# One step of a hybrid decoder on eight cores: rows transposed once and kept on chip, sample attention in small units, cache copies moved to the FFN

## Chip, cores, metric

The kernel runs on all 8 cores of one Trainium2 chip (two dies of four cores). The metric is the device time of the slowest core in microseconds (us). The four runs of the kernel before agree within 0.3% (2707.73 to 2713.84 us). Engines: PE is TensorE (PEld its weight loads), DVE is VectorE, ACT is ScalarE, POOL is GpSimd, SP is SyncE; with a "q" behind it, an engine's name stands for its issuing of instructions and DMAs. SBUF and PSUM are the on-chip memories in which the code places its tiles; `PS` in the code is PSUM. The granted clock is what the profile records of TensorE's clock, as a share of full speed. A unit, a slot and a pass are the program's own terms and are explained with the change.

## The reference, cut to what matters

```
BATCH, SEQ, D_MODEL = 4, 2048, 2048; DEC_BATCH, DEC_SEQ = 32, 4
DIL_GROUPS = ((128, 1), (512, 4), (2048, 16))   # (window, dilation), 4 heads of 128 each
D_CONV, CONV_WIDTH, FFN_HIDDEN = 1024, 31, 5632

h = rms_norm(x, g_mix)
z = h @ w_in                                    # [glu | q | k | v | gate_conv | gate_attn]
u = glu[..., :D_CONV] * sigmoid(glu[..., D_CONV:])
q, k = rope(...), rope(...)                     # rotary on 32 of 128 columns
conv_out = silu(layer_norm(depthwise_conv31(u))) @ w_pw
o_att = attention of 3 dilated groups, combined by their softmax denominators
        # prompt: each position and 128 earlier ones at stride 1, 4, 16
        # sample: 4 new rows per sequence against the cache; returns the caches shifted by 4 rows
x = x + (gate_conv * conv_out + gate_attn * (o_att @ w_o_att)) @ w_out
x = x + (silu(hf @ w_gate) * (hf @ w_up)) @ w_down     # hf = rms_norm(x)
```

A core takes 1024 prompt positions with 1024 earlier ones as halo (their keys and values are computed again), and four sample sequences (16 rows).

## The kernel before: the parts concerned

For every 128-row block of every group, the rows of x are loaded again, normalised and transposed, and Q, K, V are projected one after the other. The helper `S` records every operation for its engine and derives waits from the regions of SBUF and PSUM that an operation touches.

```python
def do_norm(idx):
    norm_tile(src, skey, hblk, 'hblk')
    ...
    issue_xload(nl)                       # next block's rows of x, stride d
    if bi_ >= 4:
        issue_copy_piece()                # cache copies, beside the x loads
        issue_copy_piece()

def do_block(idx, cur):
    ...
        do_norm(nxt)
    if has_q:
        proj(7, hTb[xi], hkey, 2)         # 16 matmuls of 512 columns each
    proj(0, hTb[xi], hkey, 0)
    proj(1, hTb[xi], hkey, 1)
    ...                                   # rope, casts, transposes of q and k
    do_T(nxt)                             # 16 transposes of the next block's rows
    for ki, (kbuf, mi) in enumerate(keyblocks):
        for h in range(4):
            S.op('pe', ... matmul(PS[sb_], lhsT=kT, rhs=qT ...))
            S.op('pe', ... matmul(PS[sb_], lhsT=identb, rhs=mb ...))   # the mask
        S.op('act', ... AF.Exp ...)
    ...

for idx, (g, bi_, r, b, kind) in enumerate(allblocks):
    if bi_ == 0:
        wload(2, w_in[...Q of g...]); wload(0, ...K...); wload(1, ...V...)
    do_block(idx, cur)
# then: sample attention, a stage of its own (VectorE passes of 2048 columns)
# then: for t in range(10): a3_norm(t) ...   rows loaded, normalised, transposed once more
# then: GLU and convolution, layer norm, gates, output projection, FFN
```

The waits come from this rule, which is the same in both kernels. Note the divisions by 32: two writes into different partitions of the same group of 32 count as a conflict.

```python
def region(self, ap):
    ...
    q0, q1 = p0 // 32, (p0 + ap.ap[0][1] + 31) // 32
```

The softmax here doesn't subtract the row's maximum and nothing guards it: scores larger than these inputs give would overflow.

## Time and profile before

| | before |
|---|---|
| time | 2708.93 us in the median of four (2707.73 to 2713.84) |
| setup and prompt attention | 0 to 737 us |
| sample attention | 737 to 905 us |
| second normalisation and transposition | 905 to 960 us |
| GLU and convolution | 960 to 1213 us |
| layer norm | 1213 to 1278 us |
| gates, wait for output weights, output projection, FFN | 1278 to 2709 us |

The boundaries are read from the timeline at the first and last instruction of each stage. The lines behind them are in the prediction below: the slices, the windows of these stages and the chain of waits. The share of busy time over the whole span (PE 84%) says little here; each stage has its own limit.

### The profile page before, as it was taken

Reading aid. Unit: us, or ns where it says so; the run is one execution under the profiler, and the core shown is the slowest. Engines: PE = TensorE matmul, PEld = TensorE weight load, DVE = VectorE, ACT = ScalarE, POOL = GpSimd, SP = SyncE. Lnnn points to the kernel's source line nnn. Section 1 sums busy time; section 2 is a strip of 40 time slices with the busy share of each in tenths; the row PEclk is TensorE's granted clock in tenths of the full one; section 3 lists DMA queues with packets and bytes.
Section 4 is the critical chain, followed back from the end, with each engine's and each line's share of the span. In section 5 each row is a group of like instructions: output and inputs, shape, how many; then the busy total and the mean of one; then the engine's idle time right before and its main releaser. Section 6 shows DMA issues by size and latency. Waiting matters only on the chain.

```text
span 2708.9 us, 36511 instructions; the slowest of 8 cores (2694.7 to 2708.9 us)
## 1 busy us (share of the span) xinstructions
PE 2277.3 (84%) x14139; PEld 1285.9 (47%) x14139; DVE 940.9 (35%) x1417; ACT 569.9 (21%) x1035; POOL 121.4 (4%) x123
## 2 busy tenths in 40 slices
PE   1894885798744389997999949999999999999997
PEld 0451443344311245554666624556555665556663
DVE  1441533354477532214222212432333223332215
ACT  1451432343432421115111101300000000000012
POOL 0000000000000000000110000000000000000000
PEclk9996997898956589998999979999999999999999
DMA  9598799694364413330546576555535546446413
GB/s 196 116 188 135 162 200 183 128 202 128 58 150 150 149 18 47 46 47 1 68 64 84 75 191 85 84 87 76 81 63 76 80 65 91 64 66 91 63 32 126
DMA packets 207406, 272.00 MB, mean 100 GB/s; under 512 B 5785, under 2 KB 185369, under 8 KB 196255
## 3 DMA queue, kind: packets, MB, share of 16 engines
q0 software_dynamic: 185712, 127.93, 34.0%
q1 hardware_dynamic: 21525, 141.74, 20.5%
q8 instruction: 115, 1.88, 0.3%
q14 instruction: 54, 0.44, 0.1%
HBM read 381.86 MB, written 59.99 MB: 163 GB/s over the span
## 4 chain that ended last, share of the span: by engine, by line
PE 78%; DMA 9%; DVE 5%; ACT 4%; issue 3%; another core or an unknown queue 1%; SPq 0%; ACTq 0%; DVEq 0%; POOLq 0%
PE ps L219 78%; DMA t_62<-w_in 3%; DMA t_69<-xext 2%; DMA wf_151<-w_out 2%; DVE t_99 L219 1%; DVE t_106 L219 1%; DMA t_59<-vecs 1%; DVE t_97 L219 0%; DMA t_117<-xext 0%; ACT t_89 L219 0%; ACT t_124 L219 0%; ACT t_71 L219 0%; ACT junk__179 L219 0%; ACT t_73 L219 0%
## 5 line engine op out<-in xcount | busy, mean ns | idle before, releaser
L219 PE MATMUL ps<-t_113,t_61 128*128 128x347 bf16 (+3 forms) x1152 | 186.6, 315 | 1.2 <-ACT t_143 L219 1.2
L219 PE MATMUL ps<-t_113,t_62 128*128 128x347 bf16 (+3 forms) x1152 | 183.4, 312 | 0.0
L219 ACT ACTIVATE sgb_177<-ps 128x347 f32<-128x347 f32 (+1 forms) x66 | 30.3, 459 | 537.8 <-PE ps L219 537.8
L219 PEld LDWEIGHTS ps<-t_113,t_61 128*128 128x128 bf16 x1152 | 112.4, 98 | 63.7 <-issue 1.8
L219 PEld LDWEIGHTS ps<-t_113,t_62 128*128 128x128 bf16 x1152 | 111.6, 97 | 60.1
L219 PE MATMUL ps<-t_61,t_72 128*128 128x512 bf16 x320 | 79.2, 405 | 45.9 <-DMA t_61<-w_in 45.0
L219 PE MATMUL ps<-t_142,wh_161 128*128 128x347 bf16 (+1 forms) x576 | 93.3, 316 | 0.5 <-DVE t_142 L219 0.5
L219 PE MATMUL ps<-t_63,t_73 128*128 128x512 bf16 x288 | 70.5, 402 | 25.5 <-DMA t_63<-w_in 21.9
L219 PE MATMUL ps<-t_142,wh_162 128*128 128x347 bf16 (+1 forms) x576 | 91.3, 312 | 0.0
L219 PE MATMUL ps<-t_142,wh_159 128*128 128x347 bf16 (+1 forms) x576 | 90.9, 311 | 0.0
L219 PE MATMUL ps<-t_142,wh_160 128*128 128x347 bf16 (+1 forms) x576 | 90.9, 311 | 0.0
L219 ACT ACTIVATE sgb_178<-ps 128x347 f32<-128x347 f32 (+1 forms) x66 | 30.3, 459 | 279.3 <-PE ps L219 279.3
L219 PE MATMUL ps<-t_62,t_72 128*128 128x512 bf16 x320 | 77.2, 397 | 12.1 <-DMA t_62<-w_in 12.1
L219 PE MATMUL ps<-t_61,t_73 128*128 128x512 bf16 x320 | 74.5, 387 | 9.4 <-DMA t_61<-w_in 7.5
L219 PE MATMUL ps<-t_114,t_63 128*128 128x347 bf16 (+1 forms) x384 | 66.7, 314 | 18.3 <-ACT t_114 L219 18.3
L219 PE MATMUL ps<-t_62,t_73 128*128 128x512 bf16 x320 | 75.1, 390 | 6.6 <-DMA t_62<-w_in 6.6
L219 PE MATMUL ps<-t_142,wh_157 128*128 128x347 bf16 (+1 forms) x480 | 75.7, 311 | 0.0
L219 PE MATMUL ps<-t_142,wh_158 128*128 128x347 bf16 (+1 forms) x480 | 75.7, 311 | 0.0
L219 PE MATMUL ps<-t_142,wh_156 128*128 128x347 bf16 (+1 forms) x480 | 75.7, 311 | 0.0
L219 PE MATMUL ps<-t_142,wh_155 128*128 128x347 bf16 (+1 forms) x480 | 75.7, 311 | 0.0
L219 PEld LDWEIGHTS ps<-t_61,t_72 128*128 128x128 bf16 x320 | 32.7, 103 | 89.0 <-issue 55.9
L219 DVE SCALAR_TENSOR_TENSOR t_71<-t_69,t_56,t_59 128x2048 bf16<-128x2048 f32 x19 | 44.7, 2352 | 86.4 <-ACT t_56 L219 86.4
(359 smaller groups left out, 3790.2 us busy)
## 6 DMA issues: line engine op xcount, KB each, us to landing
t_69<-xext SPq DMA_DIRECT2D x19, 1024.0 KB, 10.4
t_70<-xext SPq DMA_DIRECT2D x18, 1024.0 KB, 14.8
t_61<-w_in POOLq DMA_DIRECT2D x12, 1024.0 KB, 12.4
t_62<-w_in POOLq DMA_DIRECT2D x12, 1024.0 KB, 15.9
kso<-ck SPq DMA_DIRECT2D x8, 1016.0 KB, 23.1
vso<-cv SPq DMA_DIRECT2D x8, 1016.0 KB
t_63<-w_in POOLq DMA_DIRECT2D x3, 2048.0 KB, 29.0
t_61<-w_in POOLq DMA_DIRECT2D x3, 2048.0 KB, 38.5
```

The source lines that it names most:

```text
L219: self.q[eng].append(lambda e: getattr(e, meth)(*a, **kw).then_inc(s, 1))
```

## The change

Its intent is to give TensorE less to do and nothing to wait for in the first 1213 us. The 1024 own rows, the halo and the sample rows are normalised and transposed once, into `hT`, and stay on chip for all later stages. Each group becomes a pass for Q (its result kept as `qT`) and a pass for K and V, with masks as VectorE multiplies; a pass is a loop over blocks of 128 rows, and a slot is a place in such a loop at which other work may be put. The sample rows' Q, K, V are three matmuls side by side in column tiles. Sample attention is cut into 51 units (17 per group), each with its loads, three VectorE passes of 512 columns, one exponential and one matmul, spread over later stages: units 0 to 16 (group 0) run in group 1's passes, 17 to 33 in group 2's, 34 to 50 in the GLU stage. The cache copies are issued during the FFN. The core of the diff:

```diff
-        hblk = ab(o, 1024); o += 1024
-        hTb = [v3(ab(o, 1024), 16), v3(ab(o + 1024, 1024), 16)]; o += 2048
+        hT = v3(ab(H_, 16 * HP), 16)              # all rows, transposed, for all stages
...
+        def u_load(u):
+            if kind == 'n':                       # the new rows among themselves
+                for dst, r0, key in ((K_, 16, 1), (V_, 32, 2)):
+                    S.dma('sp', dst[0:64, :], ...)
+                for i_ in range(4):
+                    S.dma('sp', Q_[16 * i_:16 * i_ + 16, :], ...)
+                return
+            S.dma('sp', Q_, sq[4 * s + i:4 * s + i + 1, :].partition_broadcast(128), ...)
+            if g > 0 or i == 0:
+                S.dma('sp', K_, ck[g][s]...)
+                S.dma('sp', V_, cv[g][s]...)
+        def u_dve(u):
+            S.op('dve', ... tensor_tensor(out=P_, in0=K_, in1=Q_, op=ALU.mult))
+            S.op('dve', ... tensor_reduce(out=S_, in_=v3(P_, 4), axis=AX.X, op=ALU.add))
+            S.op('act', ... activation(out=pc, in_=S_, func=AF.Exp, scale=SCALE))
+            S.op('dve', ... tensor_tensor(out=v3(PV_, 4), in0=v3(V_, 4), in1=..pc.., op=ALU.mult))
+        def unit_slot(lim):                       # matmul of one unit, loads of the next, VectorE of one
...
+        def slotA0(i):                            # group 0: rows still to be normalised
+            if i < 6:
+                norm(11 + i)
+            if i < 7:
+                T(10 + i, 0, 7)                   # transposition into bank 7, then a copy on VectorE
+        def slotB0(i):
+            if i < 7:
+                T(10 + i, 1, 7)                   # same bank, copy on ScalarE
...                                               # GLU and convolution, per channel block n, slot ti
                     S.op('act', ... AF.Sigmoid ...)
                     S.op('dve', ... scalar_tensor_tensor(...))
                     if ti == 0:
                         S.op('dve', ... out=dg[ui] ...)   # 31 diagonals, 3968 columns
+                    unit_slot(50)
+                    if n == 1 and ti == 0:
+                        prompt_norm()             # reciprocal, then 8 x (matmul, multiply)
...                                               # FFN
+        def copy_slot():
+            slots[0] += 1
+            if slots[0] % 2 == 0 and copies:
+                d_, s_ = copies.pop(0)
+                S.dma('act', d_, s_)
```

## The prediction

> **What bounds the kernel now.** I read the page's slices first, to find where TensorE is not dense; then the windows view with boundaries I set at the stage changes that the timeline shows; then the chain of waits, for what fills the gaps; last the DMA queues.
>
> ```profile
> PE   1894885798744389997999949999999999999997
> PEclk9996997898956589998999979999999999999999
> DMA  9598799694364413330546576555535546446413
> ```
>
> One digit is 68 us. The right two thirds are a wall of nines at full clock. The losses are in the left third: slices 0, 3 to 6, and above all 11 to 14. In the windows below (busy us and count per engine, then clock, DMA share, GB/s) the first four are setup and the prompt attention of the groups 0, 1, 2; then sample attention; a second norm and transpose of the rows; GLU and convolution; gates; the wait for the output weights; the FFN without its last down round.
>
> ```profile
> 0.00:72.00 72.00, 9.12 (x35) 4.28 (x35) 10.67 (x16) 8.26 (x12) 3.76 (x7) 0.99 0.96 187
> 72.00:258.00 186.00, 138.32 (x905) 72.94 (x906) 62.52 (x130) 71.04 (x120) 3.43 (x3) 0.89 0.84 159
> 258.00:491.00 233.00, 172.25 (x1068) 90.06 (x1067) 88.50 (x167) 82.51 (x137) 3.43 (x3) 0.89 0.88 170
> 491.00:737.00 246.00, 213.24 (x1376) 110.12 (x1376) 109.64 (x237) 101.24 (x174) 4.17 (x4) 0.95 0.52 125
> 737.00:905.00 168.00, 72.92 (x258) 20.99 (x259) 118.50 (x63) 50.17 (x96) 0.40 (x1) 0.60 0.53 139
> 905.00:960.00 55.00, 17.85 (x168) 15.44 (x165) 28.12 (x18) 33.73 (x52) 0.00 (x0) 0.50 0.44 158
> 960.00:1213.00 253.00, 239.48 (x1546) 131.66 (x1546) 57.21 (x58) 29.35 (x75) 12.41 (x12) 0.98 0.31 39
> 1278.00:1573.00 295.00, 295.00 (x1999) 194.12 (x1999) 75.84 (x141) 42.25 (x94) 24.67 (x25) 1.00 0.53 67
> 1573.00:1617.00 44.00, 7.30 (x43) 3.90 (x40) 3.06 (x6) 0.86 (x2) 3.42 (x3) 0.64 0.95 249
> 1740.00:2635.00 895.00, 889.76 (x5574) 531.85 (x5574) 278.92 (x440) 64.12 (x138) 59.64 (x60) 1.00 0.50 75
> ```
>
> The chain (start, us, what) names what fills the gaps: at each change of group some 45 us for the weights plus 25 us for rows of x queued beside them; in sample attention one VectorE pass after the other.
>
> ```profile
> 169.87 13.76 PE ps L219 x97
> 211.86 43.98 DMA t_62<-w_in
> 377.73 23.52 DMA t_69<-xext
> 443.31 47.57 DMA t_62<-w_in
> 611.44 28.97 DMA t_69<-xext
> 779.99 2.30 DVE t_99 L219
> ```
>
> So TensorE bounds everything from 960 on (but for the wait of 44 us), TensorE and DMA share the attention, VectorE bounds 737 to 905, and a latency chain bounds 905 to 960.
>
> ```profile
> q0 software_dynamic: 185712, 127.93, 34.0%
> q1 hardware_dynamic: 21525, 141.74, 20.5%
> ```
>
> These two give transfer rates for saturated engines: casting weight loads 127.93 MB in 0.340 x 2709 = 921 us, 139 GB/s of bf16 (2.1 MB of weights cost 15 us); plain transfers 141.74 MB in 555 us, 255 GB/s (a 1 MB tile 4.1 us). I use them below.
>
> [...] The timeline has 16 such matmuls from 189.20 to 192.65 us, 0.2157 each[...]
> [...] mean clock 0.60 and 0.50 in the two stages with an idle TensorE. [...] 1.00 in gates and FFN with eight cores busy.
> [...] The change reads weights at strides 4 and 16; nothing before does, so the trace is silent.
> [...] x tiles land in 10.4 and 14.8 us in the median, against 5.0 us outside attention.
>
> **The change part by part.**
> *Rows normalised and transposed once.* 40 tiles in attention plus 10 before the convolution become 17. The stage 905 to 960 goes: **-55 us**. In attention 24 x 16 transposes at 0.055 us go, about 20 us of TensorE, and 21 reads of 1 MB of x.
>
> *Attention stages, rebuilt.* A projection is 16 x 0.2157 = 3.45 us. Before there are 37 K, 37 V, 32 Q and 9 sample projections (115); after 37 K, 37 V, 24 Q and three packed sample ones (48 matmuls of 32 columns; those of the FFN, 15 in 1.24 us, are packed the same way, so about 5 us each with their rope). 192 mask matmuls become VectorE multiplies. From the block of 13.76 us plus 1.3 us stall (period 15.05) I take small matmuls at 0.055 us.
> - q block: 3.45 + 4 transposes = 3.7 us. Its VectorE share: rope 0.9 (0.28 to 0.36 per op), copy 0.4.
> - full K/V block: 6.9 + 28 small x 0.055 = 8.5 us; g2 block (64 queries) 7.7; a block without queries 7.2.
> - VectorE per K/V block, with masks, rope, sums and one sample unit: 5.5 us, under the 8.5.
>
> *Group 0.* To the end of the q pass, DMA must bring three weights (45 us) and about 12.3 MB of x, gain and tables (48 us): 93 us, more than TensorE's 8 x 4.6 us. I take 92. Then 9 blocks x 8.5, 7 with a tile to transpose (0.9): 85, plus 5: **ends at 182** (before 258).
> *Group 1.* W0 is loaded early, W1 and W2 wait for the last block and take 30 us, while eight sample units bring 8 x 0.79 MB = 25 us: 54 us for a q pass that needs 30 on TensorE. Then 8 x 8.5 + 4 x 7.2 = 98, plus 5: 157, **ends at 339** (491).
> *Group 2.* 54 + 16 x 7.7 + 5 = 184, **ends at 523** (737).
> *Sample attention.* The 168 us stage goes. A unit has three VectorE passes over 512 f32 columns, a quarter of the 2.29 us passes each, 0.6, and waits 0.7 for the exponential: 2.6 us, 51 times, beside TensorE. On TensorE it costs one matmul of 0.22.
> *GLU and convolution.* 8 x 31 = 248 as before, + 17 units x 0.22 = 4, + normalising the prompt sums (8 f32 matmuls of 0.86, each with a VectorE pass of 0.69 and two handovers: 15, + reciprocal 3), + state transposes and last block 6: **276, ends at 799** (1213).
> *Sample normalisation, layer norm.* 65 + 7 = 72: 871 (1278).
> *Gates, wait for output weights, output projection, FFN.* Same instructions and the same buffer order: 295 + 44 + 123 + 969 = 1431: **2302**.
> *Cache copies.* 43.8 MB (2 x 4 x 2676 rows of 2 KB) leave attention and go, 172 us of DMA, into 8 of 11 FFN rounds of 85.5 us. The DMA share there goes from 0.50 to 0.75. Weights are loaded nearly a round ahead and land in 9 to 13 us, so I count nothing for it. For cold restarts of the clock and handovers not counted I add 13: **2315 us**.
>
> **The rivals.**
> *DMA latency becomes VectorE's wait.* Units load only one ahead, and VectorE takes its work in order: a unit whose keys are late holds up the rope, and so TensorE. For: three 256 KB loads per 3.7 us are 210 GB/s, beside weight loads. Against: only 16 slots lie in q passes; the K/V slots have 7 to 8 us. If each such slot takes 9 us: +35, 2350.
> *Strided weight loads become the bound.* The 512 loads of group 2 step 32 bytes. Contiguous loads keep up with 55 ns transposes, so a fourfold penalty just fits under 216 ns; more than that would add 50 to 100 us: 2365 to 2415.
> *The copies starve the FFN.* If loads double in latency and some arrive late: +20 to +60. Against it are the 0.75 and the slack of most of a round.
> *Gain hidden anyway.* If attention is DMA-bound throughout, fewer matmuls save little: from 0 to 523 there are 18.9 MB of weights (136 us) and by my estimate 46 MB of plain traffic (x 18, caches 10.5, queries 9, outputs 6.6, tables 2: 180 us), 316 of 523 us. So not on average, only at the group changes.
>
> **Range and chances.** The end of the convolution moves from 1213 to 799 (-414); layer norm gives back 7 and the allowance 13: -394, 2709 to 2315. Of it 223 us are two whole stages whose work has other engines' time to go to, which is why I am sure of the sign. Uncertain are the three q passes (each +-15), the GLU additions (+-12), strides (+0 to 60), copies (+0 to 50). Most errors make it longer: low 2260, high 2400. Slower or equal would take 340 us of new waits: faster 0.98, within 2% 0.015, slower 0.005.
>
> **What would show it right or wrong.** Right: attention ends at 500 to 560; no stage in which VectorE alone is dense; half clock only in the first 30 us, short spells at the group changes, layer norm and the output-weight wait; the FFN takes 969 us at clock 1.00 with a DMA share near 0.75; q passes of groups 1 and 2 near 54 us with W1 or W2 ending the wait. Wrong: weight loads of group 2 longer than 0.2 us with blocks over 8.5 us; VectorE waiting for cache keys inside K/V passes; waits for gate, up or down weights in the FFN.

## The result and the profile after

The changed kernel is correct. Of its four runs two were fast, at 2487.62 and 2488.5 us; the others (2542.23 and 2641.25 us) slow. Executions in which one die ran at a lower clock are left out of the means. The ratio to the kernel before is 0.9182, with a 95% interval from 0.9159 to 0.9204. A ratio here is the mean time of one kernel's fast runs over the mean of the other's in the same rounds, so it is not quite the ratio of medians. The kernel is 8.2% faster, 221 us; the forecast was 394 us, and the result lies outside the range of 2260 to 2400 us, 172 us above its centre.

The slices of the changed kernel (2487 us, so 62 us each), the counterpart of those in the prediction:

```profile
PE   3775996997577889699997598999999999999997
PEclk9888998998788899799999799999999999999999
DMA  9435427737132107047573956998889798544603
```

The gates, with which the dense wall begins, should have started at 871 us, in slice 14 (counted from 0); they start in slice 16, after a stretch of 5 to 8 in slices 10 to 14 in which the DMA row shows 0 to 3. No stage is VectorE's alone any more, and in the FFN, from slice 25 to 33, the DMA row rose to 7 to 9 with PE still at 9.

The windows of the same stages (us; busy and count of PE, PEld, DVE, ACT, POOL; clock; DMA share; GB/s): group 0's Q pass and K/V pass; group 1's start and rest; group 2's start and rest; the start of the GLU stage and its rest; the FFN.

```profile
39.00:105.00 66.00, 45.83 (x287) 23.70 (x285) 33.10 (x57) 29.92 (x49) 0.00 (x0) 0.88 0.77 176
105.00:218.00 113.00, 95.73 (x666) 49.77 (x667) 39.45 (x76) 41.92 (x72) 3.43 (x3) 0.91 0.30 72
218.00:260.00 42.00, 13.75 (x79) 6.56 (x78) 8.22 (x21) 3.29 (x8) 0.00 (x0) 0.67 0.90 162
...
387.00:424.00 37.00, 12.30 (x67) 6.07 (x66) 8.71 (x20) 2.33 (x6) 0.06 (x1) 0.68 0.98 171
424.00:591.00 167.00, 163.92 (x956) 102.79 (x955) 84.69 (x216) 28.22 (x70) 6.84 (x6) 0.98 0.50 107
591.00:666.00 75.00, 40.83 (x227) 21.53 (x225) 21.04 (x26) 16.33 (x24) 0.00 (x0) 0.77 0.61 109
666.00:973.00 307.00, 241.73 (x1328) 120.24 (x1328) 81.60 (x94) 59.44 (x96) 10.11 (x10) 0.86 0.23 45
...
1517.00:2412.00 895.00, 889.80 (x5574) 531.74 (x5574) 278.11 (x441) 64.13 (x138) 59.12 (x60) 1.00 0.74 124
```

The two dense passes (424 to 591, and the one before 387) are what the forecast promised (in the one before 387, from 260 us on, PE is busy for 126.55 of 127 us). Four windows are not: the K/V pass of group 0, the starts of groups 1 and 2 at a clock of two thirds, and above all the GLU stage, 382 us instead of 276, with TensorE at 0.77 and 0.86 of its clock although the DMA engines are busy to 0.61 and 0.23 only.

The chain of waits at the starts of groups 1 and 2 (start, us, what):

```profile
218.93 17.34 DMA t_67<-sqkv
236.99 6.69 DMA t_67<-sqkv
243.74 4.96 DMA t_67<-sqkv
...
467.55 12.80 DMA t_64<-ck
```

Where before 45 us for weights and 25 us for rows of x stood, there are now three loads in a row of the sample queries, `t_67`, 64 rows of 2 KB in all. They belong to the first unit of each group, the "new rows" unit, whose Q tile is written by four DMAs of 16 partitions. By the rule quoted above, the second waits for the first and the fourth for the third, because each of these pairs lies in one group of 32 partitions; the third is issued right behind the second, so three waits follow each other. The last line is a later wait, for a key tile of the cache, inside group 2's K/V pass. At the start of the GLU stage the same three take 13.36, 6.02 and 5.08 us.

Inside the GLU stage the timeline of one slot reads (start, us, engine, line, operation, operands, count, idle time before it and what ended that):

```profile
828.88 4.28 DVE L212 TENSOR_TENSOR t_105<-t_44,t_50 128x3968 bf16<-128x3968 bf16 x1
833.21 0.69 DVE L212 TENSOR_TENSOR t_69<-t_63,t_67 128x512 f32<-128x512 f32 x1
834.77 1.28 ACT L212 ACT_TABLE_LOAD   x1 [6.50 <-DVE t_75 L212]
836.28 1.28 ACT L212 ACT_TABLE_LOAD   x1
837.21 0.58 PE L212 MATMUL ps<-t_71,t_49 128*32 128x512 bf16 x1 [5.62 <-DVE t_71 L212]
```

VectorE first builds the 31 diagonals, 4.28 us, and only then starts the unit. ScalarE has to load the table of the exponential for the unit's four columns and, right behind it, the table of the sigmoid again. The unit's matmul stands in TensorE's order ahead of the next projection, so TensorE idles 5.62 us for it. The groups of table loads in the two kernels give the count:

```profile
L219 ACT ACT_TABLE_LOAD x8 | 10.3, 1283 | 36.1 <-PE ps L219 34.6 <-DVE t_137 L219 1.3
```

```profile
L212 ACT ACT_TABLE_LOAD x42 | 53.9, 1283 | 158.7 <-PE ps L212 78.0
```

The first is before (8 loads), the second after (42): the 34 that came to it are two for each of the 17 units of the GLU stage. ScalarE is 17% busy in the page of the changed kernel; that row hides them.

In the K/V pass of group 0, the timeline shows once per block:

```profile
132.79 0.67 PE L212 MATMUL ps<-t_44,t_61 128*128 128x128 bf16 x8 [3.02 <-DVE t_55 L212]
```

These eight transpositions write the PSUM bank whose former content VectorE has yet to copy; that copy (0.68 us, at 131.96) is queued behind a normalisation's multiply (2.35 us, at 129.69), which itself waits for ScalarE (2.85 us of idle time before it). After TensorE's 3.02 us of idle time the granted clock is 0.51, from 133.2 to 136.7 us, and the next projection takes 5.28 us instead of 3.63.

By stage, in us (forecast as lengths of the stages in the prediction; measured on the slowest core):

| stage | before | forecast | after | miss |
|---|---|---|---|---|
| start to the end of group 0 | 258 | 182 | 218 | +36 |
| group 1 | 233 | 157 | 169 | +12 |
| group 2 | 246 | 184 | 204 | +20 |
| sample attention, second normalisation | 223 | 0 | 0 | 0 |
| GLU and convolution | 253 | 276 | 382 | +106 |
| layer norm | 65 | 72 | 77 | +5 |
| gates to the end | 1431 | 1431 | 1437 | +6 |
| allowance | | 13 | | -13 |
| | 2709 | 2315 | 2487 | +172 |

### The profile page after: what moved, and what is told of

Same layout as the page of the kernel before. It is cut to its first block, busy times and chain, and to the rows that moved or that the text cites.

```text
span 2486.9 us, 34422 instructions; the slowest of 8 cores (2471.8 to 2486.9 us)
## 1 busy us (share of the span) xinstructions
PE 2164.7 (87%) x13264; PEld 1254.8 (50%) x13264; DVE 826.9 (33%) x1434; ACT 417.2 (17%) x789; POOL 121.6 (5%) x123
## 4 chain that ended last, share of the span: by engine, by line
PE 80%; DMA 8%; DVE 4%; issue 4%; ACT 3%; SPq 0%; DVEq 0%; ACTq 0%; POOLq 0%
PE ps L212 80%; DMA t_67<-sqkv 2%; DMA wf_141<-w_out 2%; DMA t_52<-w_in 1%; DMA t_68<-sqkv 1%; ACT L212 1%; DMA t_64<-ck 1%; DMA t_58<-xext 0%; DVE t_131 L212 0%; DVE t_130 L212 0%; ACT t_60 L212 0%; SPq L231 0%; ACT t_170 L212 0%; ACT t_112 L212 0%; DVE t_60 L212 0%
## 5 line engine op out<-in xcount | busy, mean ns | idle before, releaser
L212 PE MATMUL ps<-t_55,t_52 128*128 128x347 bf16 (+3 forms) x1152 | 189.8, 322 | 6.9 <-ACT t_133 L212 6.9
L212 PE MATMUL ps<-t_53,t_55 128*128 128x512 bf16 (+1 forms) x640 | 156.5, 401 | 6.0 <-DVE t_55 L212 6.0
L212 PE MATMUL ps<-t_55,t_53 128*128 128x347 bf16 (+3 forms) x960 | 153.7, 315 | 0.0
L212 PEld LDWEIGHTS ps<-t_55,t_52 128*128 128x128 bf16 x1152 | 115.6, 101 | 73.1 <-issue 9.1
L212 PE MATMUL ps<-t_54,t_55 128*128 128x512 bf16 (+1 forms) x640 | 145.1, 380 | 0.0
L212 PEld LDWEIGHTS ps<-t_55,t_53 128*128 128x128 bf16 x960 | 94.4, 99 | 51.1 <-issue 1.3
L212 PE MATMUL ps<-t_52,t_55 128*128 128x512 bf16 (+1 forms) x432 | 107.6, 407 | 11.8 <-DMA t_52<-w_in 11.8
L212 PEld LDWEIGHTS ps<-t_53,t_55 128*128 128x128 bf16 (+1 forms) x640 | 77.0, 126 | 68.9 <-issue 26.3
L212 PEld LDWEIGHTS ps<-t_54,t_55 128*128 128x128 bf16 (+1 forms) x640 | 76.7, 121 | 52.7
L212 ACT ACT_TABLE_LOAD x42 | 53.9, 1283 | 158.7 <-PE ps L212 78.0
L212 PEld LDWEIGHTS ps<-t_52,t_55 128*128 128x128 bf16 (+1 forms) x432 | 43.1, 104 | 63.5 <-issue 27.5
```

What stands on the lines that cost most here:

```text
L212: self.q[eng].append(lambda e: getattr(e, meth)(*a, **kw).then_inc(s, 1))
```

## The experiments

Theory: the gain was given back in four separate places: (a) the units in the GLU stage, through the alternation of tables and through their place behind the diagonals; (b) the four Q loads that wait for each other; (c) the order of copy and multiply in group 0; (d) the prompt normalisation, a chain of handovers. Rivals are the forecast's: DMA occupation, strided weight loads, starved FFN. Three kernels give a wrong sample output. "Gained" is the difference of a run's ratio to the changed kernel's 0.9182, times the 2709 us of before. The 95% intervals of the ratios are mostly 5 to 7 us wide to either side, so differences of a few us between gains mean nothing. The expectations took such differences from single runs; some of their figures differ from those here by a few us (95 us in place of 87 for the units left out).

### The units of the GLU stage left out (wrong)

```diff
-                    unit_slot(50)
+                    unit_slot(33)
...
-        while uc['pe'] < len(units):
-            unit_slot(50)
+        while uc['pe'] < 34:
+            unit_slot(33)
```

> Wrong sample output on purpose: the 17 sample units of group 2 (34 to 50) are left out, nothing else. Theory: these units are what makes the GLU and convolution stage 382 us long (591 to 973) in place of the 276 forecast: then the stage falls to about 295 us and the whole to about 2400 us (-85 to -95). Rival: the stage is long because of the normalising of the prompt sums, the state transposes and the late weights; then the time stays above 2460.

Measured: ratio 0.8861 (0.8792 to 0.8931), three fast runs from 2391.48 to 2419.6 us, so 87 us gained, give or take 19 us, because the third run is slower than the other two. The window of the GLU stage in its profile is 299 us, against 386 us with the same two boundaries (the end of attention, and the end of the sample normalisation's wait) in the changed kernel:

```profile
590.00:889.00 299.00, 256.50 (x1582) 136.93 (x1580) 72.01 (x82) 29.65 (x70) 10.11 (x10) 0.93 0.26 32
```

So the units are behind 87 of the stage's excess of about 106 us, although TensorE's own work for them is 17 matmuls. The rest remains without them.

### The units with the sigmoid in place of the exponential (wrong on purpose)

```diff
-            S.op('act', ... activation(out=pc, in_=S_, func=AF.Exp, scale=SCALE))
+            S.op('act', ... activation(out=pc, in_=S_, func=AF.Sigmoid if u >= 34 else AF.Exp, scale=SCALE))
```

> Wrong sample output on purpose: units 34 to 50 use Sigmoid in place of Exp, so that ScalarE keeps one function table in the GLU stage; the number of operations and their order are the same. Theory (table reloads): some 34 loads of 1.28 us go, four of them on the chain of each of the first six channel blocks: -29 us from the chain, with the cold clock after the stalls -30 to -50: about 2445. Rival (the units' VectorE work and its place in the queue is what counts, the loads lie in its shadow): the table loads go but the time falls by less than 10 us.

Measured: ratio 0.905 (0.9028 to 0.9072), 36 us gained with the same instructions and loads; the profile's group of table loads is back to 8. Hence 34 table loads cost 36 us, about 1.06 us each on average of the 1.283 us that one takes. In the changed kernel's chain of waits four of the six loads of a full channel block lie on the path (in the block from 757 us: at 758.68, 781.87, 790.36 and 799.38 us); for six blocks these are about 30 us, and the few us that remain are not assigned.

### The unit ahead of the diagonals

```diff
+                    unit_slot(50)
                     if ti == 0:
                         S.op('dve', ... out=dg[ui] ...)
                         S.op('dve', ... ubb ... hv ...)
-                    unit_slot(50)
```

> Correct output. The sample unit is emitted ahead of the 4.28 us VectorE pass that builds the diagonal weights, instead of after it. Theory (queue order): the chain has 3.88 + 0.23 us of this pass ahead of a unit in each of six channel blocks, on which TensorE waits 5.6 us: -20 to -30 us, about 2462. Rival (table loads alone): within 5 us of the changed kernel, since TensorE then waits for the exponential instead.

Measured: correct, ratio 0.9111 (0.9093 to 0.9128), 19 us gained. Six channel blocks each have one such slot, so 3.2 us per slot of the 4.28 us that the pass takes.

### Both edits together (wrong)

> The changed kernel with two edits of the GLU stage together, wrong on purpose: units 34 to 50 use the sigmoid function in place of the exponential (no table loads), and the unit is emitted ahead of VectorE's building of the convolution's diagonals. Alone they gave 37 and 20 us; leaving the units out gave 95. If the two causes are independent they give 57 together, 2431 us, and the 38 us that are left to the 95 belong to the units' own work and their loads at the start of the stage. If both let TensorE stand at the same place (the copies of u before the convolution), the sum is smaller, 40 us or less, 2448 us or more; if each only shifted the wait to the other, the sum is larger, 75 us or more, 2413 us or less.

Measured: ratio 0.8969 (0.8952 to 0.8987), fast runs 2433.84 to 2433.97 us, 58 us gained, against 36 + 19 = 55 alone. Within the intervals the two causes add; they are not two views of one wait. The window of its GLU stage:

```profile
590.00:926.00 336.00, 268.52 (x1571) 138.80 (x1585) 104.34 (x128) 32.62 (x87) 10.12 (x10) 0.88 0.36 67
```

It is 50 us shorter than the 386. The 37 us that still separate it from 299 can be read off the chains of waits. At the stage's start this run has 12.26 + 6.66 + 8.18 us of Q loads where the run without units waits 9.82 us for the convolution's state; at the first matmul of the prompt sums it is 20 us behind (667.27 against 647.60 us). After that, four blocks with units follow each other in 35.0 to 36.3 us against 30.9 without, 17 us more in all. No experiment separates the units' loads from their chain.

### The units moved into group 2's K/V pass

```diff
-            lim = 17 * g - 1
+            lim = 16 if g == 1 else 50
...
-            last = q_pass(g, pre, lambda: unit_slot(lim))
-            tail = kv_pass(g, last, nothing, lambda i: unit_slot(lim), after_fn(g))
+            last = q_pass(g, pre, lambda: unit_slot(min(lim, 33)))
+            tail = kv_pass(g, last, (lambda i: unit_slot(lim) if i >= 6 else None) if g == 2 else nothing,
+                           lambda i: unit_slot(lim if i > 0 or g == 1 else 33), after_fn(g))
```

> Correct output. No unit in the GLU stage: units 34 to 50 run in the K/V pass of group 2, where from the seventh block on two units run per block. Theory (the loss belongs to the GLU stage, where Exp alternates with Sigmoid and VectorE has the diagonal pass): GLU falls to about 290 us, the K/V pass of group 2 grows by at most 20 us (VectorE 3 + 2 x 2.85 = 8.7 us per block against 7.4 of TensorE, 10 blocks): about 2415 to 2430. Rival (a unit costs the same wherever it runs): the K/V pass grows by 17 x 2.85 = 48 us or more, and the whole gains under 40 us.

Measured: correct, ratio 0.8902 (0.888 to 0.8923), 76 us gained of the 87 that leaving them out gives. The GLU stage is 300 us, as without units; group 2 pays about 24 us for them, since the end of attention moves from 591 to 615 us. There the exponential is the only table in use (the whole run has 8 table loads instead of 42), and no diagonals are built.

### The four Q loads as one group

```diff
-                for i_ in range(4):
-                    S.dma('sp', Q_[16 * i_:16 * i_ + 16, :], ..., reads=[('sq', g, 0)])
+                S.dma_group('sp', [(Q_[16 * i_:16 * i_ + 16, :], ...) for i_ in range(4)],
+                            Q_[0:64, :], reads=[('sq', g, 0)])   # one semaphore, no wait between
```

> The changed kernel, correct; only the four 16-row loads of Q of a spread unit are issued as one group that ends on one semaphore, so that none waits for the one before it. Theory (the four loads wait for each other, because they write slices of one tile, and their chain of 17.3 + 6.7 + 5.0 us is what VectorE, then TensorE, stand on at the stage boundaries): the chain shrinks to one transfer of 12 to 18 us, 8 to 12 us are gained at each of the three boundaries (start of group 1, of group 2, of the GLU stage), together about 25 us: about 2462 us in the fast state. Rival (the loads are slow because they share the DMA engines with the weight loads; the order does not matter): the group takes as long as the four together, under 5 us gained, 2483 to 2488 us.

Measured: correct, ratio 0.91 (0.9073 to 0.9127), 22 us gained, give or take 7, near the theory's 25. But not evenly. The first boundary falls from 29 us of Q loads to one of 18.38 us. At the start of group 2 the chain of waits now reads:

```profile
379.40 14.85 DMA t<-sqkv
...
400.83 14.49 DMA t<-ck
...
418.13 10.84 DMA t<-cv
```

The Q loads' 27 us became 15, and then the next units' keys and values take 25 us: that boundary gains about 2 us. The DMA engines were occupied to 0.98 there in the changed kernel. So the theory holds at group 1, and at group 2 the rival fits (occupation, among others by the weights W1 and W2); no run took the weights away. At the GLU stage's start the wait falls from 24.5 to 12.58 us, but in the profiled run (2475.01 us, while two others took 2461.49 and 2462.52) the whole stage is still 386 us, at a clock of 0.80 instead of 0.84. Why the clock was lower in that run, and whether it was in the two faster ones, is not shown by a profile.

### The transposition ahead of the normalisation

```diff
-            if i < 6:
-                norm(11 + i)
             if i < 7:
                 T(10 + i, 0, 7)
+            if i < 6:
+                norm(11 + i)
```

> The changed kernel, correct; only in group 0's K/V pass the transposition of a block is emitted ahead of the next block's normalisation instead of behind it, so that the copy out of PSUM stands in front of the normalisation's multiply on VectorE. Theory (the copy queued behind the multiply makes TensorE idle 3 us per block, and the half clock that follows costs another 1.9 us): about 30 us in the seven blocks, the pass falls from 113 to about 85 us, 2458 us in the fast state. Rival (the pass is bound by the chain of the normalisation itself, ScalarE's square, logarithm and exponential, or by the loads of x; the order on VectorE only shows where the wait lands): under 8 us gained, 2480 us or more.

Measured: correct, ratio 0.9106 (0.9087 to 0.9126), 21 us gained. The pass itself did what the theory said:

```profile
105.00:195.00 90.00, 90.00 (x685) 48.27 (x684) 40.35 (x79) 42.29 (x73) 3.43 (x3) 0.97 0.45 97
```

It takes 90 us instead of 113, with no idle time on TensorE: the forecast's 85 + 5. The attention ends 26 us earlier in this profile (565 against 591 us), and the GLU stage is 401 us long, 15 more than in the changed kernel's profile, with Q loads of 29.4 us at its start (24.5 before) and a clock of 0.80 (0.84 before). So a part of what group 0 gained was lost there in this run; why is not shown.

### The kernel before with the copies in the FFN alone

```diff
             if bi_ >= 4:
-                issue_copy_piece()
-                issue_copy_piece()
...                                               # FFN, once per gate and up tile
+            copy_slot()                           # every second call: one copy, issued by ScalarE
```

> The kernel before, correct, with one part of the change alone: the cache copies are issued during the FFN. Theory (the copies fill the DMA engines during attention and are behind the waits for x of 23.5 and 29 us and a part of the waits of 44 and 47.6 us for group weights): 30 to 60 us gained, 2650 to 2680 us, FFN unchanged at about 969 us although its DMA share rises to about 0.75. Rival A (attention's waits are latency and order of issue, not occupation): within 15 us of the kernel before. Rival B (the FFN starves): slower than the kernel before, FFN above 985 us.

Measured: correct, ratio 0.9873 (0.9858 to 0.9888), 34 us gained. The same part of the chain of waits that the prediction shows of before is here:

```profile
213.03 43.98 DMA t<-w_in
430.11 41.41 DMA t<-w_in
```

The two waits for rows of x, 23.5 and 29 us, are gone: the copies delayed the rows. The wait for group 1's weights is 43.98 us as before, with the DMA engines fully busy during it in both kernels (share 1.08), so this wait does not come from the copies. From the output weights to the end the two kernels take the same 1135 us, the window of the FFN is 895 us at a clock of 1.00 with a DMA share of 0.83. So this part alone gives 34 us, against 221 for the whole change, and the FFN does not starve. Whether it gives as much inside the change was not tested.

### Four repairs together

Units in group 2's pass, grouped Q loads, transposition ahead, and the loads of the next set's first unit (unit 17) issued before group 1's passes end.

> The changed kernel, correct, with four repairs together: units 34 to 50 moved from the GLU stage to group 2's K/V pass (alone 72 us), the four Q loads as one group, group 0's transposition ahead of the normalisation, and the first loads of the next group's units issued before the group's end. If the causes are independent their gains add: 72 + 25 + 30 = 127 us, 2360 us. If they overlap (a wait removed in one place is taken up by the next: the cache keys' loads in group 2, the state load at the start of the GLU stage) less than 90 us are gained, 2400 us or more.

Measured: correct, ratio 0.8732 (0.8711 to 0.8753), 122 us gained. Alone three of them gave 76 + 22 + 21 = 119. Within the intervals they add; the fourth was not run alone, and little is left for it.

### A fifth: the prompt normalisation spread

```diff
-                        prompt_norm()
+                        prompt_recip()
+                    if n >= 2 and ti < 2 and pieces_:
+                        prompt_piece(*pieces_.pop(0))   # one matmul and one multiply
```

> The kernel with the four repairs, correct, and a fifth: the normalisation of the prompt's attention sums is spread, the reciprocal at the start of block 1 and one of the eight pairs of matmul and multiply in each of the first two slots of blocks 2 to 5, instead of all eight in a row behind the reciprocal. Theory (TensorE waits for the reciprocal, 6.7 us, and then for eight handovers to VectorE and back, 8 x 3.0 us less the matmuls' own 2.1 us at half clock): 15 to 22 us less than the kernel with four repairs, 2340 to 2346 us. Rival (the multiplies land behind the GLU's other work on VectorE and hold PSUM): under 6 us.

Measured: correct, ratio 0.8636 (0.8603 to 0.8668), fast runs 2338.41 and 2348.4 us: 26 us more than with four repairs, 148 in all. The window of the GLU stage:

```profile
567.00:846.00 279.00, 249.91 (x1591) 136.43 (x1590) 73.40 (x82) 29.87 (x71) 10.11 (x10) 0.98 0.28 39
```

279 us, where the forecast said 276; with four repairs it was 304. In the changed kernel the reciprocal takes 6.55 us and eight rounds of a matmul pair, a multiply and two handovers take 3.0 us each, 30 us, for which the forecast had 18. From 672 to 694 us the granted clock is 0.50, and a pair's matmuls take 1.13 us each, against 0.61 us spread out; the granted clock of the whole stage is 0.98 here and 0.92 with four repairs. The agreement of 279 with 276 is in part luck: the forecast's 276 holds 4 us for units, which run elsewhere here, and 18 us for the prompt sums, which are spread here, and lacks the wait for the convolution's state at the stage's start, 11.41 us in this run. This is the fastest kernel, 13.6% under the kernel before.

### The second units spread over all blocks of group 2

```diff
-    (lambda i: unit_slot(lim) if i >= 6 else None) if g == 2
+    (lambda i: unit_slot(lim) if i % 3 != 0 else None) if g == 2
```

> The kernel with five repairs, correct, with the second unit of a block in group 2's K/V pass spread over all sixteen blocks (two of every three) instead of in the last ten. Theory (in the last ten blocks each doubled block waits 5 to 7 us for the cache's keys because two units per block ask more than two buffers can prefetch; spread, every third block lets the loads catch up): 10 to 20 us less than the kernel with five repairs. Rival (the first six blocks have their DMA engines full of the GLU's weights, at a share of 1.0, so the loads only wait earlier): within 6 us of it, or slower.

Measured: correct, ratio 0.8638 (0.8619 to 0.8658), the same as 0.8636. The rival's number holds, the theory's does not. In the kernel with five repairs the chain of waits has, in group 2:

```profile
428.76 11.97 DMA t<-ck
466.53 7.79 DMA t<-ck
489.42 6.14 DMA t<-ck
```

and seven more; spread evenly, there are nine instead of ten. Placement does not help. The rival's reason is shown only in part: the DMA share is 1.01 in the first 50 us of group 2, but 0.45 to 0.74 from 465 us on, where six of the ten waits lie, and VectorE idles for the keys for 12.0 us in all from 440 us on, 3.3 us at most at a time. In the chain each of these late loads stands on SyncE's queue right behind the store of V, which waits for ScalarE's copy (487.48 the copy, 488.20 the store, 489.42 the load). Whether issuing the loads ahead of that store helps was not tried, nor was a third buffer, for which I found no free space in this layout.

## Why the prediction was wrong, point by point

The sign was right, and so were the two stages that go, the FFN and the weight loads. What failed is an overlap: the forecast took a unit's work for hidden beside TensorE in every stage, and in the GLU stage TensorE waited for it.

**GLU and convolution, "+ 17 units x 0.22 = 4": this step failed first.** It counted what a unit costs TensorE's array and nothing of what TensorE waits for. The units cost 87 us (shown by leaving them out): 36 us for 34 table loads, 19 for standing behind the diagonals, together 58 when both are removed, and, by subtraction, some 30 for their loads and the chain multiply, sum, exponential, multiply, matmul. That chain lies on TensorE's path because the matmul is queued ahead of the next projection; queueing it later was not tried. The forecast's own figure for a unit, 2.6 us on VectorE "beside TensorE", was taken for hidden in every stage. With one unit per block it was hidden in the K/V passes (PE busy for 163.92 of 167 us in group 2); with two per block it cost 24 us there, and in the GLU stage 87.

**The same sum, "normalising the prompt sums ... 15, + reciprocal 3".** Measured about 30 us, of which spreading regained 26. The reciprocal was taken as one of VectorE's usual passes, 3 us where it took 6.55, and the granted clock of 0.50 during the matmuls was left out.

**Group 0, "9 blocks x 8.5, 7 with a tile to transpose (0.9): 85, plus 5".** 113 us measured. TensorE's work was sized correctly, 90 us once the order was changed, although the terms themselves add up to 83 and not 85; what was missing is the order of two instructions on VectorE. The other 13 us of this stage's miss (the Q pass ends at 105 and not at 92) were not tested.

**Groups 1 and 2, "54 us for a q pass".** Attention ended at 591 us, outside the forecast's 500 to 560, and Q loads, not W1 or W2, end the long waits. The forecast's first rival, a late load that holds up VectorE and then TensorE, is half right: it strikes at the boundaries, and in the slots only once (12.80 us at 467.55 us, one of the prediction's own signs of being wrong). Part of it is not bandwidth but the four Q loads' waits for each other, 10 us at group 1 (shown). At group 2 the DMA engines are full, to 0.98, which fits bandwidth; for the moved units the cause is open. A second part of the miss lies in TensorE's own work, and the forecast did not have it. It counted 0.055 us for every small matmul. The score matmuls read `qT` with the group's stride; the same four, of 128 columns, in group 0 (contiguous) and in group 1 (a stride of 4 elements):

```profile
138.37 0.39 PE L212 MATMUL ps<-t_84,t_89 128*128 128x128 bf16 x4
302.54 0.62 PE L212 MATMUL ps<-t_84,t_89 128*128 128x128 bf16 x4
```

From start to start the four take 0.23 and 0.44 us, both at a granted clock of 1.00; in group 2, at a stride of 16 and with 64 columns, they take 0.47. With a unit's matmul of 0.32 us, which no block of the forecast holds, a K/V block of group 2 takes 8.45 us instead of 7.7, some 12 of the 20 us missed there.

In the kernel with five repairs the miss that is left sits in the groups: group 0 ends 12 us late, group 1 takes its 157 us, group 2 takes 215 instead of 184 (with 17 units more), GLU 279 against 276, and from there to the end 1501 us against 1503. That is 46 us less 2 less the allowance of 13: 31 over the forecast, where its profiled span of 2346.9 is 32 over.

**Strided weight loads: right to leave them out.** Weight loads of the V projection, groups by form in the changed kernel, group 1 and group 2 (busy, mean ns of one, idle time before); those of the K projection take 115 and 146 ns in the same windows:

```profile
L212 PEld LDWEIGHTS ps<-t_54,t_55 128*128 128x128 bf16 x186 | 21.2, 114 | 17.7
```

```profile
L212 PEld LDWEIGHTS ps<-t_54,t_55 128*128 128x128 bf16 x183 | 26.2, 145 | 11.6
```

A stride of 4 elements takes 114 ns, one of 16 takes 145 ns, and contiguous ones in group 0 take 98; all fit under a matmul of 216 ns, and projections of group 2 take 3.63 to 3.68 us, those of group 0 3.62 and 3.63. The rival is refuted for the weights; for the scores' moving operand, on which it says nothing, see above.

**Cache copies: right.** The forecast had 0.75 for the DMA share in the FFN and 969 us for its time; the window has 0.74, and 895 + 75 us. Alone the part gives 34 us. The prediction's chain of waits has the rows of x "queued beside" the weights; with the copies gone the two waits for x (23.52 and 28.97 us) are gone too, so the copies, issued by SyncE as the loads of x are, were behind these.

**Range.** "GLU additions (+-12)" is the term that broke it: a range of 12 on a term that was off by 106. The other misses together are +79, less the allowance +66: 2381 us, inside the upper end of 2400.

## What to carry to other kernels

Work that is spread over other stages to fill an idle engine must be priced by the stage that receives it: which function table ScalarE holds there, what stands ahead of it in each engine's order, and what stands behind its last instruction on the engine that sets the time. One small exponential among sigmoids cost two table loads, 36 us for 17 units, and moving the same units to a stage that uses the exponential anyway regained 76 of the 87 us that they cost. When a change frees several engines at once, test its parts alone: here three repairs gave 119 us alone and 122 us together with a fourth.

## More that the traces show

- Table loads: 1283 ns each (42 times in the changed kernel). In the timeline above one starts at 834.77 and the second at 836.28, with the exponential between them, and 34 loads cost 36 us in all.
- Column tiles: the sample rows' 48 matmuls of 512 columns, in three column tiles, start between 118.45 and 121.71 us, three together every 0.216 us, the time of one in a projection: about 3 times the rate of one.
- Back-to-back matmuls: full projections take 0.2157 us per matmul of 512 columns. The FFN's granted clock is 1.00 on all eight cores in the profiles of before and after, both of fast runs. In the slow runs the cores of one die show 0.79 to 0.93 over the whole run; what sets that clock is open, since no slow run was kept as a profile.
- Strides: weight loads take 98 ns contiguous, 114 at a stride of 4 bf16 elements, 145 at 16. (Contiguous ones of the K projection in group 0 show 114 too, but there those from 133.68 to 136.24 us, at a granted clock of 0.51, take 150; in the run with the transposition ahead the 580 loads of that pass take 99 in the mean.) As the moving operand of the score matmuls a stride of 4 took 0.11 us for 128 columns, against 0.057 contiguous.
- VectorE's reciprocal: 6.55 us for 128 x 1024 f32, against 0.69 us for a multiply of 128 x 512.
